# The turn of the first token half's probabilities, from the auxiliary PSUM pool to the main products' pool

## The chip, the cores and the metric

The kernel runs on one core of a Trainium2 chip. The metric is the device time of one execution in microseconds (us), given as the median of a few runs. Most executions of one kernel agree within 0.3%.

Engine names: PE is the tensor engine's matrix products and PEld its weight loads (they overlap the products), DVE the vector engine, ACT the scalar engine, POOL the GpSimd engine, SP the engine that issues most DMAs.

## What is computed

A trunk of two layers on 256 tokens of width 2048, all in float32: a Mamba-2 mixer and then an attention mixer with a sliding window of 128 tokens, four key/value heads, eight query heads to each, and a sink per head. The change lies in the attention:

```python
s = jnp.einsum("bcqhrd,bckhd->bchrqk", qb, kk) * (hd ** -0.5)
s = jnp.where(valid, s, -jnp.inf)
m = jnp.maximum(jnp.max(s, axis=-1, keepdims=True), sk)
p = jnp.exp(s - m)
p = p / (jnp.sum(p, axis=-1, keepdims=True) + jnp.exp(sk - m))
o = jnp.einsum("bchrqk,bckhd->bcqhrd", p, vv)
```

`qb` are two blocks of 128 queries; the first block sees the first 128 keys, the second sees all 256 through the window. The query projection, the gate projection, the output projection and the layer norm stand around it.

## The kernel before, in words

Large products are made of three products of float32 parts: every weight block ("unit", 128x2048) is loaded by SP in two halves of 512 KB into `wr` buffers, ACT copies it to a high part `wh` (line 160) and DVE subtracts to a low part `wl` (line 163). Units are prepared two ahead of their use (`next_unit`, line 241).

The attention layer works per key/value head j = 0..3 and token half h = 0, 1 (128 tokens each). `B_ORDER` (line 61) lists the large blocks that fill PE: `q` (query projection, products on line 972), `g` (gate projection, line 248) and `o` (output projection of an earlier head, lines 319 to 321, added to `xr` by DVE on line 326 for j = 0 and line 330 later). A block has four units, and after each unit `tick()` runs the small steps that were put off with `later(n, fn)`. So the small steps of head j stand between units of later blocks, in a fixed program order, and each engine executes its own instructions in that order.

The small steps of head j and half h:

- `qtr` (line 1047): four transposes of the queries on PE (1050), copied by ACT (1054).
- `attend` (line 1075): the scores on PE (1087). For h = 0 all four query-head pairs fit one pair of PSUM tiles; for h = 1 the keys are twice as many, so there are two pairs of tiles, four products to each pair. DVE adds the mask for h = 0 (1094); for h = 1 ACT copies (1101) and DVE overwrites by the mask (1102). Then maximum, exponentials (ACT, 1114), sums and division (DVE, 1119).
- `turn_p` (line 1123): the probabilities are turned, four transposes on PE (1127) into each of two PSUM tiles `pt`. For h = 0 the first tile is copied out by DVE (1138) and the second by ACT (1136). For h = 1 DVE multiplies each tile by two masks (1131).
- `pv` (line 1141): products with the values (1145), the gate (1151), and the split for the output projection (1160, 1161).

For j = 0, 1, 2 the steps "turn the probabilities of h = 0" and "attend h = 1" fall due at the same tick, in this order: eight transposes (1127), then the sixteen weight loads and eight products of the scores of h = 1 (1087), then the next unit's large products. This tick stands after the first unit of block q of head 1 for j = 0, and after the first unit of block o of head j - 1 for j = 1 and j = 2. For j = 3 the scores of h = 1 come one unit after those of h = 0 instead of three, and the turns of both halves stand together at a later tick.

PSUM has eight banks. `mm_tile()` (line 104) hands out the four of the main products' pool, `ax_tile()` (line 107) the four of the auxiliary pool: for scores, transposes, and `pv`. A pool hands out the buffer that has been free of recorded users for longest, and the instruction that first writes it waits on semaphores for its last readers. With `turn_p` the auxiliary pool's order at the ticks of j = 0, 1, 2 is: two tiles for the turn, two for the first pair of scores, and for the second pair of scores the two of the turn again.

Of the kernel before, what the change touches and what calls it, by code (L numbers as in the profile page):

```python
# [81 lines left out]
def trunk(ctx: ExitStack, tc: tile.TileContext, A: dict, out: bass.AP, dbg=None):  # L82
# [17 lines left out]
    def nm(s):  # L100
        uid[0] += 1
        return f"{s}_{uid[0]}"

    def mm_tile():
        return mm_ps.tile([P, 512], F32, tag="mm", name=nm("mm"), bufs=4)

    def ax_tile():
        return ax_ps.tile([P, 512], F32, tag="ax", name=nm("ax"), bufs=4)
# [966 lines left out]
    def attend(j, h):  # L1075
# [46 lines left out]

        def turn_p():
            for par in range(2):
                pt = ax_tile()
                for a in range(4):
                    nc.tensor.transpose(pt[:, a * P : (a + 1) * P], p[:, par * 4 + a, :], ident)  # L1127
                for kc in range(h + 1):
                    t = bp.tile([P, 512], F32, tag="pt", name=nm("pt"), bufs=NPT)
                    if h:  # L1130
                        nc.vector.tensor_tensor(
                            t[:].rearrange("p (a q) -> p a q", a=4), pt[:].rearrange("p (a q) -> p a q", a=4),
                            (anti, tri)[kc].unsqueeze(1).to_broadcast([P, 4, P]), ALU.mult,
                        )
                    elif par:
                        nc.scalar.copy(t[:], pt[:])
                    else:
                        nc.vector.tensor_copy(t[:], pt[:])
                    pts[kc, par] = t
# [23 lines left out]

        last = j == 3
        later(4 if last and h == 0 else 3, turn_p)
        later((5 if last else 6) if h == 0 else (8 if 0 < j < 3 else 4), pv)
        if h == 0:
# [194 lines left out]
```

## Time and profile before

| | |
|---|---|
| median of 3 runs | 998.05 us (997.94 to 998.2) |
| span of the profiled execution, first to last instruction | 996.5 us |
| so beside the span, in the runs | about 1.55 us |
| PE busy | 990.9 us, 99% of the span |
| PE weight loads busy | 899.3 us, 90% |
| DVE busy | 771.6 us, 77% |
| ACT busy | 567.2 us, 57% |
| mean granted clock of PE | 1.000 |

The page of the profile gives no total for the profiled execution beyond its span; the times that the runs report lie about 1.55 us above it. Busy time of PE is partly modelled (a product's end is not recorded), so small holes show better in the weight loads, whose rows have start times of their own. In the timeline view a row gives start, duration, engine, line, operation, what is written and read, how many instructions are merged into the row, and in brackets the idle time before it with what ended it. In the waits view a row gives who waited for whom, the total in us, how often, and the longest.

The attention layer runs from about 700 us of the span to its end.

### The profile page before, as it was taken

Reading aid. Unit: us, or ns where it says so; the run is one execution under the profiler, and the core shown is the slowest. Engines: PE = TensorE matmul, PEld = TensorE weight load, DVE = VectorE, ACT = ScalarE, POOL = GpSimd, SP = SyncE. Lnnn points to the kernel's source line nnn. Section 1 sums busy time; section 2 is a strip of 40 time slices with the busy share of each in tenths; the row PEclk is TensorE's granted clock in tenths of the full one; section 3 lists DMA queues with packets and bytes.
Section 4 is the critical chain, followed back from the end, with each engine's and each line's share of the span. In section 5 each row is a group of like instructions: output and inputs, shape, how many; then the busy total and the mean of one; then the engine's idle time right before and its main releaser. Section 6 shows DMA issues by size and latency. Waiting matters only on the chain.

```text
span 996.5 us, 17887 instructions
## 1 busy us (share of the span) xinstructions
PE 990.9 (99%) x7036; PEld 899.3 (90%) x7036; DVE 771.6 (77%) x1186; ACT 567.2 (57%) x992; POOL 106.4 (11%) x130
## 2 busy tenths in 40 slices
PE   9999999999999999999999999999999999999998
PEld 8999989999999998999999999888988878978976
DVE  7888897867886886786786787898688776676686
ACT  7595856547646645664654764565545544544542
POOL 0001202004003003000300300403000000000003
PEclk9999999999999999999999999999999999999999
DMA  9787587565576666656656456457664546546432
GB/s 364 250 281 300 168 275 213 183 221 178 181 243 184 222 196 192 212 191 210 207 172 227 152 188 219 169 169 244 234 199 144 177 155 192 154 150 200 133 145 84
DMA packets 61555, 198.81 MB, mean 200 GB/s; under 512 B 6848, under 2 KB 11360, under 8 KB 61216
## 3 DMA queue, kind: packets, MB, share of 16 engines
q1 hardware_dynamic: 58528, 188.47, 57.6%
q0 software_dynamic: 2336, 8.69, 2.6%
q8 instruction: 55, 0.90, 0.4%
q10 hardware_dynamic: 608, 0.52, 0.2%
q14 instruction: 28, 0.23, 0.1%
HBM read 195.43 MB, written 2.23 MB: 198 GB/s over the span
## 4 chain that ended last, share of the span: by engine, by line
PE 98%; DVE 1%; issue 0%; ACT 0%; DVEq 0%
PE mm L248 53%; PE mm L972 10%; PE mm L319 9%; PE mm L320 9%; PE mm L321 9%; PE ax L627 2%; PE ax L1087 1%; PE ax L1145 1%; PE ax L603 1%; PE ax L1127 1%; PE ax L586 0%; PE mm L386 0%; PE ax L1050 0%; PE ax L903 0%; DVE wl L163 0%; PE ax L368 0%
## 5 line engine op out<-in xcount | busy, mean ns | idle before, releaser
L163 DVE TENSOR_TENSOR wl<-wr,wh 128x1024 fp32r<-128x1024 f32 (+2 forms) x338 | 392.9, 1182 | 108.7 <-ACT wh L160 106.6
L160 ACT ACTIVATE wh<-wr 128x1024 fp32r<-128x1024 f32 (+2 forms) x338 | 332.6, 1010 | 208.4 <-issue 84.9
L248 PE MATMUL mm<-xH,wh 128*128 128x256 f32 x1280 | 355.7, 278 | 0.0
L248 PE MATMUL mm<-xL,wh 128*128 128x256 f32 x1280 | 354.4, 277 | 0.0
L248 PE MATMUL mm<-xH,wl 128*128 128x256 f32 x1280 | 354.2, 277 | 0.0
L248 PEld LDWEIGHTS mm<-xH,wh 128*128 128x128 f32 x1280 | 241.0, 188 | 1.8 <-ACT wh L194 0.5
L248 PEld LDWEIGHTS mm<-xL,wh 128*128 128x128 f32 x1280 | 241.0, 188 | 1.0
L248 PEld LDWEIGHTS mm<-xH,wl 128*128 128x128 f32 x1280 | 240.8, 188 | 0.0
L319 PE MATMUL mm<-wh,yH 128*128 128x512 f32 x256 | 101.4, 396 | 0.0
L320 PE MATMUL mm<-wh,yL 128*128 128x512 f32 x256 | 99.8, 390 | 0.0
L321 PE MATMUL mm<-wl,yH 128*128 128x512 f32 x256 | 99.7, 389 | 0.0
L643 POOL TENSOR_TENSOR yz<-yz,z 128x256 f32<-128x256 f32 x32 | 32.8, 1033 | 470.4 <-DVE yz L638 470.4
L248 PE MATMUL mm<-x1H,wh 128*128 128x256 f32 x256 | 71.7, 280 | 0.0
L490 DVE SCALAR_TENSOR_TENSOR cv<-mm,pc,cv 128x255 f32<-128x255 f32 x144 | 68.6, 477 | 3.3 <-ACT cv L488 1.9
L248 PE MATMUL mm<-x1L,wh 128*128 128x256 f32 x256 | 70.8, 277 | 0.0
L248 PE MATMUL mm<-x1H,wl 128*128 128x256 f32 x256 | 70.8, 276 | 0.0
L972 PE MATMUL mm<-wh,x1H 128*128 128x512 f32 x160 | 62.9, 393 | 0.0
L972 PE MATMUL mm<-wl,x1H 128*128 128x512 f32 x160 | 61.8, 389 | 0.0
L972 PE MATMUL mm<-wh,x1L 128*128 128x512 f32 x160 | 60.9, 390 | 0.0
L319 PEld LDWEIGHTS mm<-wh,yH 128*128 128x128 f32 x256 | 48.1, 188 | 10.3 <-DVE z L579 1.0
L321 PEld LDWEIGHTS mm<-wl,yH 128*128 128x128 f32 x256 | 48.1, 188 | 10.2
L320 PEld LDWEIGHTS mm<-wh,yL 128*128 128x128 f32 x256 | 48.1, 188 | 9.0
(217 smaller groups left out, 1349.6 us busy)
## 6 DMA issues: line engine op xcount, KB each, us to landing
wr<-in_wa SPq DMA_DIRECT2D x154, 512.0 KB, 5.0
wr<-in_wo SPq DMA_DIRECT2D x64, 512.0 KB, 4.2
wr<-in_wq SPq DMA_DIRECT2D x32, 512.0 KB, 4.5
wr<-in_wg SPq DMA_DIRECT2D x31, 512.0 KB, 4.9
wr<-in_wb SPq DMA_DIRECT2D x16, 512.0 KB, 4.8
wr<-in_wb SPq DMA_DIRECT2D x32, 256.0 KB, 3.6
rb<-rscr SPq DMA_DIRECT2D x11, 512.0 KB, 4.6
wr<-in_wkv SPq DMA_DIRECT2D x8, 512.0 KB, 4.5
```

The lines of the kernel that those rows point to most:

```text
L160: m = nc.scalar.activation(h[:, sl], v, AF.Copy)
L163: m = nc.vector.tensor_tensor(l[:, sl], v, h[:, sl].bitcast(F32), ALU.subtract)
L248: m = nc.tensor.matmul(ps, a, b, start=first and i == 0, stop=last and i == 2)
L319: pinned(nc.tensor.matmul(ps, aH[:, k, hs], u.h[:, ks], start=k == 0 and add is None, stop=False), pin)
L320: pinned(nc.tensor.matmul(ps, aL[:, k, hs], u.h[:, ks], start=False, stop=False), pin)
L321: pinned(nc.tensor.matmul(ps, aH[:, k, hs], u.l[:, ks], start=False, stop=k == 3), pin)
L490: nc.vector.scalar_tensor_tensor(a[:, sft:], ps[:, : S - sft], w(3 - sft), a[:, sft:], ALU.mult, ALU.add)
L603: nc.tensor.transpose(ps[:, o : o + P], st.xs[i][:, c * P : (c + 1) * P], ident)
L627: nc.tensor.matmul(ps[64 * r : 64 * r + 64, cols], xd[:, c, r, :], e[:, 256:] if c else e[:, :256], start=c == 0, stop=c == 1,)
L643: nc.gpsimd.tensor_tensor(v, v, st.z[i][:], ALU.mult)
L972: m = nc.tensor.matmul(ps[:], (x1H, x1L, x1H)[i][:, kk, hs], (u.h, u.h, u.l)[i][:, ks], start=(kk, i) == (0, 0), stop=ui == 3 and (k, i) = ...
L1087: nc.tensor.matmul(pss[par][:, i * nk : (i + 1) * nk], q2[rows, b + i, :], kT[rows, j, :nk], start=True, stop=True,)
```

## The change

One line of `turn_p`: the tile into which the probabilities are turned comes from the main products' pool when h = 0, and from the auxiliary pool as before when h = 1.

```diff
         def turn_p():
             for par in range(2):
-                pt = ax_tile()
+                pt = ax_tile() if h else mm_tile()
                 for a in range(4):
                     nc.tensor.transpose(pt[:, a * P : (a + 1) * P], p[:, par * 4 + a, :], ident)
```

Built, both kernels have the same instructions in the same order on PE, DVE, ACT, POOL and SP. What differs is the PSUM bank of eight tiles (two for each head) and of those that the pools hand out after them, and the semaphore waits that follow from the banks. At the ticks of j = 1 and j = 2 the main pool's order becomes: two tiles for the output products of the unit before, two for the turn, then for the next output products the two of the unit before again, and after these the two of the turn.

## The prediction

> **What bounds the kernel now.** I read the page first (busy shares and the chain that ended last), then the waits view of the attention layer on PE, then the timeline of the weight loads around each tick at which the changed step stands.
>
> ```profile
> PE 990.9 (99%) x7036; PEld 899.3 (90%) x7036; DVE 771.6 (77%) x1186; ACT 567.2 (57%) x992; POOL 106.4 (11%) x130
> ...
> PE 98%; DVE 1%; issue 0%; ACT 0%; DVEq 0%
> ```
>
> PE is busy 99% of the span and is 98% of the chain that ended last. So every hole on PE that is closed comes off the end, and little else does. Which holes does the attention layer have? The waits view from 735 to 988 us, weight loads only, lists them (us in total, times, longest; left out are two of 0.3 us for "issue", one before L972 and one before L248):
>
> ```profile
> PEld ax L1145 <- issue: 4.0, 13, 0.4
> PEld ax L1050 <- issue: 2.4, 3, 0.8
> PEld ax L1127 <- ACT wh L160: 1.6, 2, 0.8
> PEld mm L319 <- issue: 1.5, 3, 0.8
> PEld ax L1087 <- ACT pt L1136: 0.8, 2, 0.4
> PEld ax L1127 <- issue: 0.8, 1, 0.8
> PEld ax L1087 <- DVE pt L1138: 0.5, 1, 0.5
> PEld ax L1087 <- PE ax L1127: 0.5, 3, 0.2
> ...
> PEld ax L1145 <- DVE wl L163: 0.3, 1, 0.3
> ```
>
> Most are changes of shape on PE ("issue"). No large product (L248, L972, L319) waits for weights. What waits for another engine's result of the same tick is line 1087, the scores of h = 1: three times, for the copies of the turned probabilities (L1136, L1138). Those copies read the two banks into which the second pair of scores goes next. Here are the three ticks, j = 0, 1, 2, as the weight loads show them (start, duration, merged count, idle before):
>
> ```profile
> 739.23 0.73 PEld L1087 LDWEIGHTS ax<-kT,qT 64*128 64x128 f32 x8 [0.17 <-PE ax L1127]
> 740.49 1.13 PEld L1087 LDWEIGHTS ax<-kT,qT 64*128 64x128 f32 x8 [0.53 <-DVE pt L1138]
> 741.95 0.19 PEld L972 LDWEIGHTS mm<-wh,x1H 128*128 128x128 f32 x1 [0.33 <-issue]
> ```
> ```profile
> 792.94 1.16 PEld L1087 LDWEIGHTS ax<-kT,qT 64*128 64x128 f32 x10 [0.17 <-PE ax L1127]
> 794.52 0.73 PEld L1087 LDWEIGHTS ax<-kT,qT 64*128 64x128 f32 x6 [0.42 <-ACT pt L1136]
> 795.58 0.19 PEld L319 LDWEIGHTS mm<-wh,oH 128*128 128x128 f32 x1 [0.33 <-issue]
> ```
> ```profile
> 868.35 1.16 PEld L1087 LDWEIGHTS ax<-kT,qT 64*128 64x128 f32 x10 [0.17 <-PE ax L1127]
> 869.93 0.73 PEld L1087 LDWEIGHTS ax<-kT,qT 64*128 64x128 f32 x6 [0.42 <-ACT pt L1136]
> 870.99 0.19 PEld L319 LDWEIGHTS mm<-wh,oH 128*128 128x128 f32 x1 [0.33 <-issue]
> 871.10 0.19 PEld L320 LDWEIGHTS mm<-wh,oL 128*128 128x128 f32 x1
> 871.33 0.19 PEld L321 LDWEIGHTS mm<-wl,oH 128*128 128x128 f32 x1
> ```
>
> The reader is to see that sixteen loads of line 1087 are torn in two, and that the tear ends where a copy ends. Why the copies are late stands on DVE and ACT, here at j = 1:
>
> ```profile
> 789.32 0.41 DVE L1071 SCALAR_TENSOR_TENSOR sg<-sg,mm 128x256 f32<-128x256 f32 x1
> 789.65 1.22 DVE L163 TENSOR_TENSOR wl<-wr,wh 128x1024 fp32r<-128x1024 f32 x1
> 790.78 0.68 DVE L326 SCALAR_TENSOR_TENSOR xr<-xr,mm 128x512 f32<-128x512 f32 x1
> 792.17 0.69 DVE L326 SCALAR_TENSOR_TENSOR xr<-xr,mm 128x512 f32<-128x512 f32 x1 [0.71 <-PE mm L321]
> 792.78 0.68 DVE L1138 COPY pt<-ax 128x512 f32<-128x512 f32 x1
> 793.38 2.35 DVE L163 TENSOR_TENSOR wl<-wr,wh 128x1024 fp32r<-128x1024 f32 x2
> ```
> ```profile
> 791.99 2.00 ACT L160 ACTIVATE wh<-wr 128x1024 fp32r<-128x1024 f32 x2 [3.07 <-issue]
> 793.90 0.56 ACT L1136 COPY pt<-ax 128x512 f32<-128x512 f32 x1
> ```
>
> ACT splits two halves of a unit (2.00 us) ahead of its copy, which ends at 793.90 + 0.56 = 794.46; PE goes on at 794.52. DVE's copy ends at 792.78 + 0.68 = 793.46, before the second pair is reached.
>
> **The change part by part.** It removes no instruction and adds none; the lists of all engines stay as they are. It removes waits and adds waits.
>
> *Removed, j = 0, 1, 2:* the second pair's wait for the copies. Its two banks were last read by the mask additions of h = 0 (line 1094), a block earlier; at j = 1 these are the row below, ended by 777.94, against a need at about 794.
>
> ```profile
> 776.66 1.28 DVE L1094 TENSOR_TENSOR p<-ax,cc 128x512 f32<-128x512 f32 x2
> ```
>
> What is the tick worth without the tear? The listed idle (0.53 and twice 0.42) is not all of it: at j = 0 the second row's eight loads take 1.13 us where the first eight took 0.73, because ACT's copy holds the second tile of the pair inside that row, too short a hole to be listed. So I don't add idle times, but take the same sixteen loads where nothing tears them, which is at j = 3:
>
> ```profile
> 931.97 1.60 PEld L1087 LDWEIGHTS ax<-kT,qT 64*128 64x128 f32 x16
> 933.90 0.19 PEld L248 LDWEIGHTS mm<-x1H,wh 128*128 128x128 f32 x1 [0.33 <-issue]
> ```
>
> From the first load of the scores to the first load of the next large product: 933.90 - 931.97 = 1.93 us here, with the same 0.33 us at the end. At j = 0 it is 741.95 - 739.23 = 2.72, at j = 1 795.58 - 792.94 = 2.64, at j = 2 870.99 - 868.35 = 2.64. Gains: 0.79 + 0.71 + 0.71 = **2.21 us**. The bounds of this term: from below 1.3 us, the sum of the waits view's 0.8 and 0.5; from above 2.21 and a little for the PE instructions that carried several waits (at most three fewer to each tick, held against cadences that show no hole there, so I take nothing; 0.3 us as the upper end). I take 2.21, since the j = 3 rows are the same instructions with the same shapes.
>
> *Removed, j = 3:* the turn there had older banks and no idle before it in the list above. Nothing.
>
> *Added:* (a) The turn's second tile waits for the last gate product's evacuation (line 1071), a unit earlier; at j = 1 that ends at 789.32 + 0.41 = 789.73, 3.2 us before the scores that follow the turn begin (792.94). (b) At j = 1 and 2 the first output products after the scores (L319) take the banks of the two output products before the turn and wait for their additions, lines 326 or 330. At j = 1 these end at 790.78 + 0.68 = 791.46 and 792.17 + 0.69 = 792.86. Without the tear the first product comes at 795.58 - 0.71 = 794.87, the second twelve products later: 3.4 us and more to spare. Queued behind that L319 are all following products of PE, so a miss would cost its full length; none is due. (c) The third and fourth of these products wait for the copies themselves, 24 and 36 products after the scores: at the pitch of these loads (871.33 - 871.10 = 0.23 us) that is 5.5 and 8.3 us after 794.87, against copies done at 793.46 and 794.46. (d) At j = 0 the next user of the turn's banks is the gate block, three units on. (e) At j = 3 the first product after the turns waits for the addition of the output product two before:
>
> ```profile
> 949.88 0.68 DVE L330 TENSOR_TENSOR xr<-xr,mm 128x512 f32<-128x512 f32 x1
> ```
> ```profile
> 952.01 0.19 PEld L319 LDWEIGHTS mm<-wh,oH 128*128 128x128 f32 x1
> ```
>
> 952.01 - 950.56 = 1.45 us to spare, the least of all added waits. PE will reach it 2.21 us sooner; DVE's row there follows exponentials and splits that are themselves released by PE, so it comes sooner too. If it stayed where it is, 2.21 - 1.45 = 0.76 us would be given back. I take nothing and keep 0.76 for the range.
>
> *What is late next.* The weights: ACT's splits wait for PE to free buffers, not the other way round (of the idle time in the row below PE ended 19.6 + 2.9 us, and PE's own list has no large product that waits for a split).
>
> ```profile
> L160 ACT ACTIVATE wh<-wr 128x1024 fp32r<-128x1024 f32 x69 | 71.2, 1051 | 54.2 <-issue 30.8 <-PE mm L248 19.6 <-PE ax L1127 2.9
> ```
>
> At the end of the kernel DVE waits for the last product, so the tail moves with PE:
>
> ```profile
> 988.34 0.43 DVE L866 BATCH_NORM_STATS2 st<-mm 128x6 f32<-128x256 f32 x1 [0.80 <-PE mm L321]
> ```
>
> *The clock.* PE ran at the full granted clock through the torn tick of j = 0:
>
> ```profile
> 738.00:743.00 5.00, 4.87 (x31) 3.49 (x30) 4.97 (x9) 3.86 (x8) 1.08 (x2) 1.00 0.88 278
> ```
>
> (The third number from the end is the granted clock, 1.00.) The Trainium skill, "TensorE: Matmul & The Clock Gate", section "A second HAM failure mode: psum-queue depth-cycling", says that cycling through PSUM banks can leave PE idle for short moments often enough that its clock gate swings between full and half. The change makes the main pool cycle faster, so by that rule the clock could fall; by the rows it does not, as holes of 0.4 to 0.5 us did not lower it. The sum stays 2.21 by the rows; by the rule it is the last rival.
>
> The sum is made on the span: 996.5 - 2.21 = 994.3; the runs lie 1.55 above the span, 998.05 - 2.21 = **995.8 us**.
>
> **The rivals.** *Only the listed idle goes* (1.3 us): what the waits view doesn't list turns up again without the tear. Or (e) gives 0.76 back: 2.21 - 0.76 = 1.45. Both near 996.7. For: the waits view, which counts every idle stretch long enough to be listed, has no more. Against: the difference from first load to next product counts the short holes too.
>
> *The change does not free the second pair:* another wait ends at the same time, say the bank is still held by another reader. 998.05. Against: line 1094 is done 16 us before.
>
> *Slower:* the first output product after the scores stands on DVE's additions at j = 1 and j = 2. It decides from the point at which DVE is more than 3.4 us behind. If the pair of splits that follows the copy (2.35 us) and three more of about 1.2 us came ahead of the addition, it would end at 791.46 + 2.35 + 3.6 = 797.4, 2.5 us after 794.87; twice, 5.1 lost, 2.2 gained: 1000.9. Against it: DVE is idle for 0.71 us ahead of the second addition, waiting for PE, so it has no backlog.
>
> *The clock falls:* if after each of the three ticks one stretch as long as a 24-product unit (24 x 0.23 = 5.5 us) ran at half clock, 16.5 us would be lost, 1012. Nothing in the rows speaks for it.
>
> **How the numbers follow.** About 0.2% (2.0 us, below 996.05) is what a measurement of this kernel can tell from no change, and the forecast lies just beyond it. Forecast 995.8: 0.69, of which 0.63 below 996.05 and 0.06 above. Only part of the gain, 996.7: 0.18. No gain: 0.08. Slower by DVE: 0.04. Clock: 0.01. So faster 0.63, same 0.06 + 0.18 + 0.08 = 0.32, slower 0.05. The range: low 995.3 = 998.05 - 2.21 - 0.3 and 0.2 for scatter; high 996.9 = 998.05 - 1.3 and 0.2; it leaves out the last three cases, 0.13, and a little at the edges.
>
> **What would show it.** In the profile after, the sixteen loads of line 1087 at j = 0, 1, 2 should be one row, 1.93 us from the first to the next large product, with no idle ended by L1136 or L1138; the loads of L319 after them should follow their 0.33 us without a new wait; the start of those ticks should move by 0, 0.8 and 1.5 us and the last product by 2.2. It is wrong if L319 shows idle ended by L326, L330 or the copies, if the rows stay apart, or if the granted clock falls.

## The result, and the profile after

The changed kernel takes **996.0 us** (median of 21 executions, 995.05 to 998.85) beside 997.95 us (median of 21, 997.07 to 1000.18) of the kernel before: 1.95 us less, ratio 0.998 with an interval of 0.9974 to 0.9987. By that interval the gain is 1.3 to 2.6 us. The profiled execution took 995.49 us with a span of 993.4 us.

Busy times and the shares of the chain that ended last, from the page of the changed kernel:

```profile
PE 987.9 (99%) x7036; PEld 897.4 (90%) x7036; DVE 772.0 (78%) x1186; ACT 566.8 (57%) x992; POOL 106.0 (11%) x130
...
PE 99%; DVE 0%; DVEq 0%; issue 0%
```

PE is still the bound, and the 1% of DVE that the chain had is gone. DVE, ACT and POOL do the same work in the same busy time (within 0.4 us). PE's fell by 3.0 us and that of its weight loads by 1.9; a busy time of PE holds small holes.

The weight loads of the changed kernel at j = 0, 1, 2, timeline view (start, duration, merged count, idle before and what ended it):

```profile
738.29 1.60 PEld L1087 LDWEIGHTS ax<-kT,qT 64*128 64x128 f32 x16 [0.17 <-PE mm L1127]
740.22 0.19 PEld L972 LDWEIGHTS mm<-wh,x1H 128*128 128x128 f32 x1 [0.33 <-issue]
```
```profile
791.21 1.60 PEld L1087 LDWEIGHTS ax<-kT,qT 64*128 64x128 f32 x16 [0.17 <-PE mm L1127]
793.13 0.19 PEld L319 LDWEIGHTS mm<-wh,oH 128*128 128x128 f32 x1 [0.33 <-DVE wl L163]
```
```profile
865.93 1.60 PEld L1087 LDWEIGHTS ax<-kT,qT 64*128 64x128 f32 x16 [0.17 <-PE mm L1127]
867.86 0.19 PEld L319 LDWEIGHTS mm<-wh,oH 128*128 128x128 f32 x1 [0.33 <-DVE wl L163]
```

The reader is to see one row of sixteen where there were two, and 1.93, 1.92 and 1.93 us from its start to the next large product, where there were 2.72, 2.64 and 2.64. DVE at j = 1 (timeline view) shows why nothing new stops PE:

```profile
789.05 0.67 DVE L326 SCALAR_TENSOR_TENSOR xr<-xr,mm 128x512 f32<-128x512 f32 x1
790.44 0.69 DVE L326 SCALAR_TENSOR_TENSOR xr<-xr,mm 128x512 f32<-128x512 f32 x1 [0.71 <-PE mm L321]
791.05 0.68 DVE L1138 COPY pt<-mm 128x512 f32<-128x512 f32 x1
```

The copy (L1138) is no earlier within the tick than before; only nobody on PE stands on it any more. The addition that the first L319 now waits for ended at 789.05 + 0.67 = 789.72, 3.41 us ahead of 793.13. The waits view of the weight loads from 735 to 988 us (total, times, longest), the rows that bear on it:

```profile
PEld mm L319 <- issue: 0.8, 1, 0.8
PEld mm L319 <- DVE wl L163: 0.7, 2, 0.3
PEld ax L1087 <- PE mm L1127: 0.5, 3, 0.2
```

No wait of L1087 for a copy is left. The two waits of L319 for L163 are the 0.33 us after the scores at j = 1 and 2, which the list of before put under "issue": another name for a gap of the same length, and at j = 0, where the profile names nothing, it is 0.33 too.

Where did the 3.1 us between the two spans (996.5 and 993.4) come from? The first load of line 972 and the last of line 321 enclose the attention layer's large products; this stretch is called the stage below. (Line 972 also makes the key and value products ahead of head 0, so the layer begins near 662 us and not at 700.) Before:

```profile
662.47 0.19 PEld L972 LDWEIGHTS mm<-wh,x1H 128*128 128x128 f32 x1
```
```profile
987.90 0.19 PEld L321 LDWEIGHTS mm<-wl,oH 128*128 128x128 f32 x1
```

After:

```profile
661.53 0.19 PEld L972 LDWEIGHTS mm<-wh,x1H 128*128 128x128 f32 x1
```
```profile
984.77 0.19 PEld L321 LDWEIGHTS mm<-wl,oH 128*128 128x128 f32 x1
```

The stage took 325.43 us and now takes 323.24: **2.19 us** less. The other 0.94 us was there before the stage began, in a part that the change doesn't touch. The experiments say whether that belongs to the change: of those without a gain, first_tile_only starts the stage late and copy_twice_aux and scores_first start it early (below), so the start doesn't go with the gain. Where in the start-up it arises is told in the last section.

### The profile page after: what moved, and what is told of

Read it like the earlier page. It is cut to its first block, busy times and chain, and to the rows that moved or that the text cites. A ratio compares the mean times of both kernels' runs of the same rounds, so it can differ in the third digit from the quotient of the medians.

```text
span 993.4 us, 17887 instructions
## 1 busy us (share of the span) xinstructions
PE 987.9 (99%) x7036; PEld 897.4 (90%) x7036; DVE 772.0 (78%) x1186; ACT 566.8 (57%) x992; POOL 106.0 (11%) x130
## 4 chain that ended last, share of the span: by engine, by line
PE 99%; DVE 0%; DVEq 0%; issue 0%
PE mm L248 53%; PE mm L972 11%; PE mm L319 9%; PE mm L320 9%; PE mm L321 9%; PE ax L627 2%; PE ax L1087 1%; PE ax L1145 1%; PE ax L603 1%; PE ax L586 0%; PE mm L386 0%; PE ax L1050 0%; PE ax L1127 0%; PE mm L1127 0%; PE ax L903 0%; PE ax L368 0%
## 5 line engine op out<-in xcount | busy, mean ns | idle before, releaser
L163 DVE TENSOR_TENSOR wl<-wr,wh 128x1024 fp32r<-128x1024 f32 (+2 forms) x338 | 393.0, 1182 | 106.7 <-ACT wh L160 104.6
L319 PE MATMUL mm<-wh,yH 128*128 128x512 f32 x256 | 101.4, 396 | 0.0
L972 PE MATMUL mm<-wh,x1H 128*128 128x512 f32 x160 | 62.9, 393 | 0.0
L972 PE MATMUL mm<-wl,x1H 128*128 128x512 f32 x160 | 61.8, 389 | 0.0
L972 PE MATMUL mm<-wh,x1L 128*128 128x512 f32 x160 | 60.9, 389 | 0.0
L319 PEld LDWEIGHTS mm<-wh,yH 128*128 128x128 f32 x256 | 48.1, 188 | 10.3 <-DVE z L579 0.9
```

The lines of the kernel that those rows point to most:

```text
L163: m = nc.vector.tensor_tensor(l[:, sl], v, h[:, sl].bitcast(F32), ALU.subtract)
L319: pinned(nc.tensor.matmul(ps, aH[:, k, hs], u.h[:, ks], start=k == 0 and add is None, stop=False), pin)
L972: m = nc.tensor.matmul(ps[:], (x1H, x1L, x1H)[i][:, kk, hs], (u.h, u.h, u.l)[i][:, ks], start=(kk, i) == (0, 0), stop=ui == 3 and (k, i) = ...
```

## The experiments

**Theory.** PE's scores of h = 1 stand behind the *place of the copies in the queues of DVE and ACT*, through the bank that a copy holds. The last copy out of a bank (ACT's, behind two splits) sets the end of the tick; take both copies out of that pool, and the tick falls to 1.93 us whatever the copies do. **Rivals:** each of the two tiles carries half of the gain; or the gain comes from the order of the main pool or from another wait that the new banks happen to drop, and the copies' time has nothing to do with it.

In the table, "tick" is from the first load of L1087 to the next large product at j = 0, 1, 2, "stage" is as above, "start" the first load of L972, all from the timeline of one profiled execution; medians and ratios are of timed runs beside the kernel before. The experiments are told in turn below it.

| kernel | tick j = 0, 1, 2 (us) | start | stage | median (us), before's | ratio (interval) |
|---|---|---|---|---|---|
| before | 2.72, 2.64, 2.64 | 662.47 | 325.43 | | |
| changed | 1.93, 1.92, 1.93 | 661.53 | 323.24 | 996.0, 997.95 | 0.998 (0.9974-0.9987) |
| first_tile_only | 2.72, 2.64, 2.64 | 662.39 | 325.44 | 998.1, 997.98 | 1.0 (0.9991-1.0009) |
| second_tile_only | 2.32, 1.93, 1.93 | 661.56 | 323.61 | 996.22, 997.98 | 0.998 (0.9972-0.9989) |
| copy_twice_aux | 3.49, 3.25, 3.26 | 661.63 | 327.44 | 1000.29, 997.98 | 1.0022 (1.0013-1.0031) |
| copy_twice_main | 1.93, 1.93, 1.93 | 661.54 | 323.25 | 996.24, 997.98 | 0.9983 (0.9974-0.9991) |
| copies_earlier | 2.26, 2.18, 2.18 | 662.07 | 324.11 | 997.56, 998.35 | 0.9996 (0.9987-1.0005) |
| scores_first | 1.93, 1.93, 1.93 | 661.67 | 328.19 | 1000.76, 998.35 | 1.0023 (1.0015-1.0032) |
| both_halves_main | 1.93, 1.93, 1.93 | 661.71 | 324.81 | 997.39, 998.35 | 0.9989 (0.9981-0.9998) |
| five_and_three | 2.32, 1.93, 1.93 | 692.56 | 323.60 | 1029.52, 998.35 | 1.0309 (1.0295-1.0323) |

### One tile at a time

```diff
-                pt = ax_tile()
+                pt = mm_tile() if h == 0 and not par else ax_tile()   # first_tile_only
+                pt = mm_tile() if h == 0 and par else ax_tile()       # second_tile_only
```

> Only the first of the two turned tiles of h = 0 (the one that DVE copies) goes to the main pool; the one that ACT copies stays in the auxiliary pool, and its bank becomes that of the fourth score tile. Theory: PE waits for the last copy out of a bank that the scores need, and that is ACT's; so the tick (first load of the h = 1 scores to first load of the next large product) stays at 2.72, 2.64 and 2.64 us and the gain is 0.0 us. Rival: two main-pool banks relieve the auxiliary pool in proportion, so one tile of two gives half, ticks near 2.3 us and 1.1 us gained. Second rival: the gain seen in the profile was only an earlier start, then no tick depends on this.

> Only the second tile (the one that ACT copies) goes to the main pool; the one that DVE copies stays, and its bank becomes that of the fourth score tile. Theory: the score pair would reach that bank 0.76 us after the tick's start. At j = 1 and 2 DVE's copy is done by then (793.46 against 793.69 in the trace of before), so these ticks fall to 1.93 us; at j = 0 it is not (740.43 against 739.98), and the tick falls only from 2.72 to about 2.3 us. Gain 0.4 + 0.7 + 0.7 = 1.8 us. Rival: half of the whole, 1.1 us, ticks near 2.3 us at all three.

The first tile alone, which DVE copies out, gains nothing; the second alone, which ACT copies out, gains 325.43 - 323.61 = 1.82 us of the 2.19. At j = 0 with the first tile moved:

```profile
738.51 0.47 PEld L1127 LDWEIGHTS ax<-cc,p 128*128 128x128 f32 x4
739.15 1.16 PEld L1087 LDWEIGHTS ax<-kT,qT 64*128 64x128 f32 x10 [0.17 <-PE ax L1127]
740.81 0.73 PEld L1087 LDWEIGHTS ax<-kT,qT 64*128 64x128 f32 x6 [0.51 <-ACT pt L1136]
```

DVE's copy no longer stops PE, and the row simply runs on to the tile behind ACT's copy. With the second tile moved, at j = 0:

```profile
738.32 1.99 PEld L1087 LDWEIGHTS ax<-kT,qT 64*128 64x128 f32 x16 [0.17 <-PE mm L1127]
740.64 0.19 PEld L972 LDWEIGHTS mm<-wh,x1H 128*128 128x128 f32 x1 [0.33 <-issue]
```

One row, without a listed wait, and yet 1.99 instead of 1.60 us long: a hole inside a merged row, here from DVE's copy. At j = 1 and 2 DVE's copy ends before the second pair is reached, and the row is 1.60. So the rival of two halves falls: of two waits that stand one behind the other, the later one has nearly all of the gain, and the earlier one has some only after the later is gone (0.39 us at j = 0).

### The copy's length, in the old banks and in the new

```diff
                     elif par:
-                        nc.scalar.copy(t[:], pt[:])
+                        for _ in range(2):
+                            nc.scalar.copy(t[:], pt[:])
```

ACT's copy is done twice, in the kernel before (copy_twice_aux) and in the changed one (copy_twice_main).

> The kernel before, but ACT copies its turned tile out twice in a row (the same values again), so that the bank is held for one copy more, about 0.47 us. Theory: each tick grows by it, to about 3.1 us at j = 1 and 2 and to 3.2 or 3.3 at j = 0, where a copy of scores stands between the two; 1.5 us slower than before in all. Rival, that the copies are not what PE waits for: ticks unchanged at 2.7 and 2.6 us.

> The changed kernel with the same doubled copy. Theory: in the main pool the bank is needed again only 8 us later, so the longer hold costs nothing: ticks 1.93 us, 2.2 us faster than before and 3.7 us faster than the same doubling in the auxiliary pool. Rival, that the main products pay for a late copy: a wait before a product of line 319 after the tick, and 0.5 us lost at j = 1 and 2.

ACT at j = 0 of copy_twice_aux, and the loads there:

```profile
739.44 0.56 ACT L1137 COPY pt<-ax 128x512 f32<-128x512 f32 x1
739.91 0.37 ACT L1101 COPY p<-ax 128x256 f32<-128x256 f32 x1
740.17 0.59 ACT L1137 COPY pt<-ax 128x512 f32<-128x512 f32 x1
```
```profile
738.39 0.73 PEld L1087 LDWEIGHTS ax<-kT,qT 64*128 64x128 f32 x8 [0.17 <-PE ax L1127]
739.66 0.73 PEld L1087 LDWEIGHTS ax<-kT,qT 64*128 64x128 f32 x4 [0.53 <-DVE pt L1139]
740.82 0.73 PEld L1087 LDWEIGHTS ax<-kT,qT 64*128 64x128 f32 x4 [0.43 <-ACT pt L1137]
741.88 0.19 PEld L972 LDWEIGHTS mm<-wh,x1H 128*128 128x128 f32 x1 [0.33 <-issue]
```

The second copy ends at 740.17 + 0.59 = 740.76, and PE goes on at 740.82. The ticks grow by 0.77, 0.61 and 0.62, the stage by 2.01 us. In the changed kernel the same copies end as late, and the ticks stay at 1.93 and the stage at 323.25:

```profile
740.08 0.59 ACT L1137 COPY pt<-mm 128x512 f32<-128x512 f32 x1
```
```profile
738.30 1.60 PEld L1087 LDWEIGHTS ax<-kT,qT 64*128 64x128 f32 x16 [0.17 <-PE mm L1127]
740.23 0.19 PEld L972 LDWEIGHTS mm<-wh,x1H 128*128 128x128 f32 x1 [0.33 <-issue]
```

This is the pair that decides: the price of the copy's time is there with the old banks and zero with the new. The rival that the copies have nothing to do with it falls. At +2.0 us in the stage, where 1.5 was expected, the miss on the old banks was one of size: the first copy of the scores (L1101) slipped between the two copies at j = 0, and at j = 1 and 2 the second copy cost 0.61 us and not 0.47. Both kernels also have some 0.5 us more between the last product's load and the end (9.1 us for 8.6). It doesn't come from the copies. In these two, in the kernel before and in the changed one alike, DVE's last instruction ends 5.74 us after that load and the last transfer of the output is issued 5.80 us after it. That transfer then lands after 2.4 us and not 1.9; copies_earlier and five_and_three, without a doubled copy, have a longer end too (9.35 and 9.14 us).

### The copies one place earlier in the queue

```diff
-                    elif par:
+                    elif True:
                         nc.scalar.copy(t[:], pt[:])
```

In the kernel before, ACT copies both tiles of h = 0 out; in the built order both copies then stand behind one split instead of two. The edit so also takes the first tile's copy off DVE.

> The kernel before, with both copies of the turned h = 0 tiles on ACT, which then stand behind one weight split of the tick's two and not behind both. All tiles stay in the auxiliary pool. Theory: the tear ends with the last copy, wherever the tile lies, so an earlier copy shortens it: by the trace of before the second copy would end near 794.0 and not 794.46 at j = 1, so the ticks fall to about 2.15 us at j = 1 and 2, and to about 2.3 at j = 0; 1.4 us gained without any change of bank. Rival, that the pool matters and not the time of the copy: ticks as before, 2.7, 2.6, 2.6.

ACT at j = 0:

```profile
737.87 1.15 ACT L160 ACTIVATE wh<-wr 128x128 fp32r<-128x128 f32 x2 [3.07 <-issue]
738.93 1.05 ACT L1136 COPY pt<-ax 128x512 f32<-128x512 f32 x2
739.88 1.07 ACT L160 ACTIVATE wh<-wr 128x1024 fp32r<-128x1024 f32 x1
```

The copies are through at 738.93 + 1.05 = 739.98 and the ticks shrink to 2.26, 2.18 and 2.18: 1.32 us less in the stage, near the 1.4 expected, with the banks of before. So in these ticks the bank matters through the time at which its copy ends. The timed runs (-0.79 us in the median, 0.9987 to 1.0005) can't be told from no change; this verdict rests on the trace alone, whose span is only 1.0 us shorter than that of before, since the end is 0.7 us longer, as said above.

### The scores ahead of the turn

```diff
+        if h == 0 and not last:
+            later(3, lambda: attend(j, 1))
         ...                                     # turn_p and pv put off as before
-        if h == 0:
-            later(1 if last else 3, lambda: attend(j, 1))
+        if h == 0 and last:
+            later(1, lambda: attend(j, 1))
```

> The kernel before, with the scores of h = 1 ahead of the turn of h = 0 in the tick, for j = 0, 1, 2; all in the auxiliary pool. Theory: now the turn needs the banks of the first score pair, whose last reader is DVE's masked overwrite (line 1102), behind ACT's splits and copies and DVE's splits; the hole moves in front of the turn and grows to about 2 us at each tick, 3 to 5 us slower than before. Rival, that the hole comes from the order turn, scores itself: 2 us faster, as with the change.

The scores are untorn, but the turn, now behind them, takes banks that the scores' readers hold. Loads at j = 0, and the waits view from 735 to 1000 us:

```profile
737.55 1.60 PEld L1087 LDWEIGHTS ax<-kT,qT 64*128 64x128 f32 x16 [0.35 <-PE mm L972]
739.48 0.19 PEld L972 LDWEIGHTS mm<-wh,x1H 128*128 128x128 f32 x1 [0.33 <-issue]
741.58 0.86 PEld L1127 LDWEIGHTS ax<-cc,p 128*128 128x128 f32 x8 [1.92 <-DVE p L1102]
```
```profile
PEld ax L1127 <- DVE p L1102: 5.3, 3, 1.9
```

The stage is 2.76 us longer, a little less than the 3 to 5 expected: about 5.3 us of new waits, less the 2.2 us of the tears that are gone. In both orders the four auxiliary banks are too few for this tick; the order decides which of the two steps waits, on whom and how long.

### Both halves in the main pool

```diff
-                pt = ax_tile()
+                pt = mm_tile()
```

> The changed kernel, with the turn of h = 1 in the main pool as well. Theory: the h = 1 turn had no wait for a bank, so nothing more is gained, and its copies are done before the main pool comes round: ticks 1.93 us and the stretch from the first product of line 972 to the last of line 321 stays at 323.25 us within 0.2. Rival: four more tiles to each head make the large products wait, 0.5 us or more lost.

My expectation of no difference from the change failed, and the rival named there held: the stage is 324.81 us, 1.57 more than with the change. The 1.57 us stand at two places. Aligned product by product with the changed kernel, 0.93 us come at the turn of j = 3, where both halves stand together (loads, then DVE):

```profile
947.82 1.46 PEld L1127 LDWEIGHTS mm<-cc,p 128*128 128x128 f32 x12
950.08 0.42 PEld L1127 LDWEIGHTS mm<-cc,p 128*128 128x128 f32 x4 [0.80 <-ACT wh L160]
```
```profile
947.55 0.68 DVE L330 TENSOR_TENSOR xr<-xr,mm 128x512 f32<-128x512 f32 x1
948.15 1.22 DVE L163 TENSOR_TENSOR wl<-wr,wh 128x1024 fp32r<-128x1024 f32 x1
949.29 0.68 DVE L330 TENSOR_TENSOR xr<-xr,mm 128x512 f32<-128x512 f32 x1
```

Four tiles in a row use up all four main banks, so the last one needs the bank of the output product just ahead of it, whose addition stands behind a split on DVE and ends at 949.29 + 0.68 = 949.97; PE goes on at 950.08. The view names ACT's split as the releaser; by the times I read the addition, since that split row runs on until 948.45 + 2.10 = 950.55 on ACT:

```profile
948.45 2.10 ACT L160 ACTIVATE wh<-wr 128x1024 fp32r<-128x1024 f32 x2 [2.24 <-PE mm L1127]
```

The other 0.6 us is a gate product behind the turn of j = 0, h = 1, which waits for the query projection to be read out:

```profile
759.43 0.19 PEld L248 LDWEIGHTS mm<-x1H,wh 128*128 128x128 f32 x1 [0.60 <-DVE qt L1044]
```

So the pool that is right for h = 0 is wrong for h = 1: the banks that were taken there are freed late.

### Five auxiliary banks and three main ones

```diff
-        return mm_ps.tile([P, 512], F32, tag="mm", name=nm("mm"), bufs=4)
+        return mm_ps.tile([P, 512], F32, tag="mm", name=nm("mm"), bufs=3)
-        return ax_ps.tile([P, 512], F32, tag="ax", name=nm("ax"), bufs=4)
+        return ax_ps.tile([P, 512], F32, tag="ax", name=nm("ax"), bufs=5)
-        pss = [mm_tile() for _ in range(NF + 1)]
+        pss = [ax_tile()] + [mm_tile() for _ in range(NF)]
```

> The kernel before with five banks in the auxiliary pool and three in the main pool (one of the four tiles of the first products moves with them); the turn stays auxiliary. Theory: with five banks the last score tile meets the bank of the first turned tile, which DVE copies, so the ticks are those of the kernel with only the second tile moved: 2.32, 1.93, 1.93 us; from line 972's first product to line 321's last 323.6 us if three main banks cost nothing there. What three banks cost in the first layer is open, estimated at 0 to 3 us. Rival, that main products with three banks pay in the attention layer: waits of L319 or L972 of 0.5 us or more there.

In the attention layer it did what was expected, to the hundredth: one more bank frees the tile behind ACT's copy, and the ticks and the stage are those of second_tile_only. But 31 us are lost before that layer (its start is at 692.56), where I had put 0 to 3. The waits view of the weight loads from 0 to 690 us, the first three rows:

```profile
PEld mm L248 <- DVE xr L328: 17.3, 5, 4.1
PEld mm L319 <- issue: 3.3, 9, 1.2
PEld mm L248 <- DVE z L579: 3.1, 2, 2.1
```

With three main banks the Mamba layer's products wait for DVE's additions (first row). A second part is the granted clock (the third number from the end) of the 100 us stretches; here the fourth:

```profile
300.00:400.00 100.00, 97.07 (x732) 91.31 (x732) 70.53 (x94) 51.85 (x77) 9.44 (x11) 0.98 0.57 187
```

The clock stands at 0.98 in the first five stretches and at 1.00 in the same stretches of the changed kernel. The 0.98 is a mean of two levels. Here are the end of the longest wait (timeline view) and, 1.5 us later, a window of 3.4 us (windows view):

```profile
280.14 0.19 PEld L248 LDWEIGHTS mm<-xH,wh 128*128 128x128 f32 x1 [4.06 <-DVE xr L328]
```
```profile
281.60:284.98 3.38, 3.38 (x18) 3.38 (x17) 3.38 (x5) 0.28 (x1) 0.00 (x0) 0.50 0.50 155
```

In this window the granted clock is 0.50, and the loads take 0.33 us instead of 0.19. The same is found behind four other waits of 2.07 to 3.35 us, beginning 0 to 1.5 us after they end (at 27.75, 191.51, 366.23 and 452.24); behind a sixth, of 3.27 us (538.59), the clock stays at 1.00. At half clock 17 loads stand in 3.38 us, behind the sixth wait 30 in 3.41 us, so each of the five windows costs about 1.5 us by an estimate from these rows, 7.5 us together. With the 23.7 us of the three waits above that makes 31.2, beside the 31.0 by which the layer starts later. That the waits bring the clock down is read from the order in time; no run tests it by itself.

No kernel of these beats the change.

## Why the prediction was right

*The mechanism* (the second score pair waits for banks that late copies hold) stands on three legs: the torn rows are gone, one doubled copy costs 2.01 us in the old banks and nothing in the new, and an earlier copy returns 1.32 us without any new bank.

*The size.* The 2.21 us, taken from the untorn row at j = 3 rather than from listed idle, measured 2.19 us in the stage (ticks 0.79 + 0.72 + 0.71). The 1.95 us of the medians are less, but their interval (1.3 to 2.6) holds both, so the choice between 2.2 and 1.3 us rests on the traces. There the rival "only the listed idle goes" (1.3 us) falls: the difference lay in short holes inside merged rows, as second_tile_only shows with one row of 1.99 us beside 1.60.

*The added waits.* All stayed within their slack. The first L319 at j = 1 had 3.41 us where 3.4 was worked out. The tightest, at the turn of j = 3, kept its slack, since DVE's row moved with PE: of the 0.76 us kept for the range nothing was lost. The addition and the product of the changed kernel:

```profile
946.75 0.68 DVE L330 TENSOR_TENSOR xr<-xr,mm 128x512 f32<-128x512 f32 x1
```
```profile
948.89 0.19 PEld L319 LDWEIGHTS mm<-wh,oH 128*128 128x128 f32 x1
```

948.89 - 947.43 = 1.46 us, where it was 1.45. That this slack is real and not large is what both_halves_main shows: two more tiles in the same pool at this tick cost 0.93 us.

*The tail.* The last product came 2.19 us sooner relative to the stage's start, and the end followed it: 993.4 - 984.77 = 8.63 us beside 996.5 - 987.90 = 8.60.

*The clock.* From 660 to 985 us, where the stage lies, the granted clock of the changed kernel is 1.00 (mean over the span 0.999). The rule of the Trainium skill, "TensorE: Matmul & The Clock Gate", section "A second HAM failure mode: psum-queue depth-cycling", didn't decide here: three ticks with one more turn of the pool are no steady cycling, and PE stood on no added wait. In five_and_three, where PE does wait again and again for main banks, the clock swings between 1.00 and 0.50, as by that rule; why one of six waits has no half clock behind it, the runs don't show.

*The total.* It came out close partly by offset: the span was 993.4 where 994.3 was worked out (0.94 us of start-up that isn't the change's), and the profiled execution lay 995.49 - 993.4 = 2.09 above its span where 1.55 had been taken from a span and a median of different executions. That the median fell on the near side of the 996.05 of the forecast, by 0.05 us, is less than the scatter can tell. Counted from the stage's start, the ticks begin 0, 0.79 and 1.48 us sooner (76.76 for 76.76, 129.68 for 130.47, 204.40 for 205.88), as expected (0, 0.8, 1.5).

## What to carry to other kernels

A PSUM bank is held until its copy has come through the queue of the engine that makes it, so a short copy (here 0.56 us) behind long splits (2.00 us) can stop PE two steps further on; give such a tile banks from the pool whose next user is due latest, and work out that user's slack, tile by tile. Price a tear by the same instructions where they run untorn, not by the idle that a view lists: merged rows hide short holes. When two waits stand one behind the other, removing the earlier alone is worth nothing.

## What was unexpected on the chip

- One main bank fewer cost 31 us of 998 (three banks for four), of which the largest part (17.3 us) is PE behind DVE's additions. Behind five of the six waits of over 2 us the granted clock was 0.50 for 3.4 us, although PE was busy again.
- The start of the program differs by 0.94 us between the profiled executions, one of each kernel (start of the attention layer 661.53 to 662.47, five_and_three left out), half the size of the effect under study. In the profiled execution of before the first weight loads take 0.33 us until 6.65 us of the span, in that of the changed kernel they take 0.19 from 4.87 on, while the view gives a granted clock of 1.00 for both; the first two rows are of before, the third of the changed kernel:

```profile
5.16 0.33 PEld L248 LDWEIGHTS mm<-xH,wh 128*128 128x128 f32 x1
...
6.65 0.33 PEld L248 LDWEIGHTS mm<-xL,wh 128*128 128x128 f32 x1
```
```profile
4.87 0.19 PEld L248 LDWEIGHTS mm<-xH,wl 128*128 128x128 f32 x1
```

Loads of 0.33 us are those of the half-clock windows of five_and_three. So PE most likely started at half clock in both and kept it some 2 us longer in the execution of before; the view's 1.00 doesn't speak against it, since the clock records of the traces begin only at 7.03 us (before) and 4.85 us (changed), where the loads turn to 0.19. By 7.97 and 7.33 us, the start of the next row of loads (L386) in each, 0.64 of the 0.94 us are there; from 35 us on the distance stays at 0.94. Another start-up shows another cause: first_tile_only has loads of 0.19 us from 4.49 on and starts the layer at 662.39; PE waits there 0.42 us for the next DMA of `first` (at 7.62) and 0.45 us for ACT's split of it (at 8.27). The rest wasn't taken apart.
